# A hybrid decoder layer: GpSimd's elementwise work handed to VectorE and ScalarE in three stages, a factor read from PSUM, and copies moved behind a load

## The chip, the cores and the metric

The kernel runs on one core of one Trainium2 chip. The time is the device time in microseconds of one execution; of several runs the median is taken. In the profile the engines are PE (TensorE; PEld is its loading of weights), DVE (VectorE), ACT (ScalarE), POOL (GpSimd) and SP (SyncE, which in this kernel issues all DMAs). Each engine works through its own list of instructions in order, and instructions on different engines wait for each other through semaphores.

## The reference

One layer of a hybrid decoder on 1024 tokens of width 1024, then a final RMSNorm, all in float32:

```python
h = h + concat(gated_delta_net(rmsnorm(h)), s5(rmsnorm(h))) @ w_out   # one in-projection
h = h + cross_attention(rmsnorm(h), rmsnorm(mem))                     # 4 heads, 256 memory tokens
h = h + (silu(hn @ w_gate) * (hn @ w_up)) @ w_down                    # hn = rmsnorm(h), 2816 wide
return rmsnorm(h)
```

The parts that the change touches are these. In the delta net, q, k and v pass a causal convolution of width 4 and a silu; each of 4 heads then works with gates `g` (decay) and `beta`, of which cumulative sums, `exp(g_cum)` and `exp(-|g_cum[i] - g_cum[j]|)` are needed. Its output is normalised, `o * rsqrt(mean(o*o) + eps) * gain * silu(z)`. The S5 branch ends in `y = gelu(y)`, `y = y * sigmoid(y @ w_glu + b_glu)`. The last RMSNorm multiplies each token's row by one factor and each column by a gain.

## The kernel before, in words

Activations lie with the channel on the partitions and the tokens along the row, in tiles of 128 partitions and 512 columns. Matrix products are made to keep float32's accuracy: each operand is split into a high part and a low part (`split`, L62 on ACT makes the high one, L63 on DVE or POOL the low one), and a product is three matmuls (`mm3`, L79 to L81) that accumulate in one PSUM bank. PSUM has eight banks, handed out by pools: `pm` (three banks, tiles named mm) is there all the time; `p5` (one bank, tiles named aux) until the S5 gate is done; `pda`, `pdb`, `p6`, `ps`, `po` in single stages; `pa` (five banks, aux again) from the out-projection on. A tile that is asked for while its pool's banks are in use waits until the readers of the oldest are done.

The order of the instructions on each engine isn't the order of the program text: a planner simulates the engines with its own costs and lays each instruction where it expects its inputs and its buffer to be ready. `issue_after(x)` forces what is written under it to stand behind x on x's engine. All loads and stores go through `load` (L54), so they all stand in SP's queue.

The stages, with the lines that matter:

1. The in-projection of S5's inputs, then `s5_setup` and `s5_pre`, which make each channel group's impulse response in HBM (TD). `s5_toeplitz` copies it, from HBM to HBM in eight DMAs of 256 KB, into shifted form (TT), which `s5_in` reads much later.
2. `zab` makes z and the gates' raw values; `gates` computes g and beta, sums g with two small matmuls into p5 (gc and, transposed, gr) and stores gr to HBM (gD). `mem_prep` norms the memory tokens: a column sum and a row broadcast, both in p5, and eight scalings (L826) that read that bank.
3. For each of four heads: `in_tile` projects k, q and v; its convolution (L489 to L492) accumulates in p5. `dn_a` loads gD as a broadcast to all partitions (d_Qg), subtracts on POOL (L583), takes Abs and Exp on ACT (L584 to L586), and copies two single columns, al and kdc, on DVE (L588, L589). Then come transposes (L595) and products on PE in the pool pda.
4. `dn_seq` runs the recurrence over 8 chunks of tokens; `dn_tail` (L791 to L799) norms a chunk's output: squares and sums on ACT, a reciprocal root in ten tiny DVE operations (L85 to L89), a product with the root on DVE, a product with silu(z), the tile sz, on POOL, transposes on PE. The S5 recurrence runs beside it.
5. `glu`, the S5 gate: eight products, in p5 and p6 by turns; ACT takes the sigmoid into an SBUF tile (L909), DVE adds the two halves of y (L910), POOL multiplies (L911).
6. Out-projection, cross-attention, the two wide feed-forward products.
7. The down-projection, five chunks of 512 features with Winograd's 7 products for 2 x 2 blocks. `down_acts` loads a chunk's activations, subtracts (L1255) and splits them (L63) into seven operands; of these, the splits number 1, 3, 7 and 6 and one subtraction, two tiles each, are on POOL, ten operations of 128x512 for each chunk. `down_weights` splits weights, half of them on POOL (wlo from wb). `down_products` adds each product to hT or Q on DVE (L1325).
8. The rest of the features, and the final norm, for 512, 256 and 256 tokens. `final` broadcasts the factor with matmuls (L143) into a PSUM bank, copies it to SBUF on ACT (L139), and multiplies eight tiles, even ones on DVE (L1380), odd ones on POOL (L1378); a store follows each pair.

Of the kernel before, what the change touches and what calls it, by code (L numbers as in the profile page):

```python
# [9 lines left out]
F32 = mybir.dt.float32  # L10
F32R = mybir.dt.float32r
I32 = mybir.dt.int32
AF = mybir.ActivationFunctionType
ALU = mybir.AluOpType
# [4 lines left out]
P = 128  # L19
NT = 1024  # L20
HT = 512
# [24 lines left out]
class Kernel:  # L46
# [478 lines left out]
    def gates(self, ab, cv):  # L525
# [25 lines left out]
        ps = self.p5.tile([P, HT], F32, name="aux")  # L551
# [5 lines left out]
        ps = self.p5.tile([P, HT], F32, name="aux")  # L557
# [8 lines left out]
    def dn_a(self, hd, q, k, dp, dx):  # L566
# [15 lines left out]
        self.load(Qg, self.gD.rearrange("(c h) p -> h c p", h=4)[hd:hd + 1].to_broadcast(sh))  # L582
# [5 lines left out]
        v.tensor_copy(out=al, in_=Qg[:, :, P - 1])  # L588
        v.tensor_copy(out=kdc, in_=E[:, :, P - 1])  # L589
# [190 lines left out]
    def dn_tail(self, c, po, dq, xs):  # L780
# [14 lines left out]
        v.tensor_tensor(out=on, in0=po, in1=ro.unsqueeze(2).to_broadcast(sh), op=ALU.mult)  # L795
        g.tensor_tensor(out=on, in0=on, in1=sz, op=ALU.mult)
# [7 lines left out]
    def mem_prep(self, cv):  # L804
# [12 lines left out]
        ps = lambda: self.p5.tile([P, HT], F32, name="aux")  # L817
# [72 lines left out]
    def glu(self, q8, xs):  # L890
# [9 lines left out]
        for h in range(2):  # L900
            yh, yl = y8[h]
            out = []
            for m in range(4):
# [4 lines left out]
                sg, yy = T("yr"), T("yy", 8)  # L908
                self.a.activation(out=sg, in_=ps, func=AF.Sigmoid, bias=self.bglu[:, m:m + 1])  # L909
                self.v.tensor_tensor(out=yy, in0=yh[:, m].bitcast(F32), in1=yl[:, m].bitcast(F32), op=ALU.add)  # L910
                self.g.tensor_tensor(out=yy, in0=yy, in1=sg, op=ALU.mult)  # L911
# [319 lines left out]
    def down_acts(self, c, raw=None):  # L1231

        v, g = self.v, self.g
# [23 lines left out]
        def first(n):  # L1257
            if n == 0:
                put(1, b11, self.g)
                put(2, b21, self.v)  # L1260
            elif n == 1:
                put(3, b22, self.g)
                sub(v, b11, b12, b11)
                sub(g, b12, b22, b12)
            elif n == 2:
                put(7, b12, self.g)
                sub(v, b22, b22, b11)
                sub(v, b21, b21, b22)

        def rest(lw):  # L1270
# [4 lines left out]
            put(6, b22, self.g)  # L1275
# [94 lines left out]
    def final(self, o, rs):  # L1370

        n = o.stop - o.start
        rb = self.tmp.tile([P, HT], F32, name="res", bufs=2)[:, 0:n]
        self.rowbc(rs, n // P, rb)
        for m in range(KD):
            dst = self.out_rows(m, o)
            if m % 2 == 1:
                self.g.tensor_tensor(out=dst, in0=dst, in1=rb, op=ALU.mult)  # L1378
            else:
                self.v.scalar_tensor_tensor(out=dst, in0=dst, scalar=self.gain(4, m), in1=rb, op0=ALU.mult, op1=ALU.mult)  # L1380
# [27 lines left out]
    def emit(self, ctx):  # L1408
# [32 lines left out]
        with pool("cv", bufs=1) as cv:  # L1441
# [12 lines left out]
            with pool("s5t", "right", bufs=1) as tp:  # L1454
# [3 lines left out]
                self.s5_toeplitz(S)  # L1458
# [4 lines left out]
            with psum("pda", 1) as self.pda, psum("pdb", 2) as self.pb:  # L1463
                with pool("dx", "right", bufs=1) as dx:
                    for hd in range(4):
                        k, q = self.in_tile(4 + hd, cv), self.in_tile(hd, cv)
                        B = self.dn_a(hd, q, k, dp, dx)
                        v_ = self.in_tile(8 + hd, cv)
# [211 lines left out]
```

## Time and profile before

| | us |
|---|---|
| median of 3 runs | 1603.62 |
| lowest and highest run | 1600.15, 1607.66 |
| the profiled execution | 1605.2 |
| its span, first to last instruction | 1603.2 |
| busy in it: PE, PEld | 1457.7, 1218.8 |
| busy in it: DVE, ACT, POOL | 1188.9, 634.7, 655.9 |

A row of the profile's groups reads: line, engine, operation, tile written and tiles read, shapes, count, then busy time in us, mean duration in ns, and the idle time of the engine just before these instructions, with what ended it. A row of a timeline reads: start, duration, engine, line, operation, tiles, shapes, count, and in brackets the idle time before it and whose work ended it. The granted clock of PE is given as a share of full speed. SPq stands for the queue of SyncE. Stretches are in us from the start of the span.

### The profile page before, as it was taken

The page shows a single profiled execution, that of the slowest core. Times are in us where ns is not written, and L with a number is a line of the kernel's source. Part 1 is how long each engine was busy: PE and PEld are TensorE (multiplying, and loading weights), DVE is VectorE, ACT ScalarE, POOL GpSimd, SP SyncE. Part 2 cuts the span into 40 slices and gives each one's busy share as a digit, 9 for nine tenths or more (in the row PEclk, how much of TensorE's full clock was granted, in tenths as well). Part 3 has the DMA queues.
Part 4 walks back from the last instruction along what each step waited for, and adds up shares of the span by engine and source line. Part 5 has one row for each costly group of instructions (what it writes and reads, how often), then busy time and mean ns, then how long its engine had stood idle before and what let it go on. Part 6 is the DMA issues. An engine that isn't in the chain of part 4 may idle for free.

```text
span 1603.2 us, 20926 instructions
## 1 busy us (share of the span) xinstructions
PE 1457.7 (91%) x7326; PEld 1218.8 (76%) x7326; DVE 1188.9 (74%) x2164; ACT 634.7 (40%) x1137; POOL 655.9 (41%) x475
## 2 busy tenths in 40 slices
PE   6887699996978788999999999999999998999985
PEld 4787488886877576878888788888888886777864
DVE  8969489886699797775546697666666668899886
ACT  5222353452544563454443442333333334533322
POOL 6175234324552416620010443333333347766544
PEclk9999899997989988999999999999999999999997
DMA  7256454548688152245524414444444357444302
GB/s 224 80 164 199 134 133 124 140 119 293 213 291 265 47 197 105 79 131 171 171 92 165 144 33 145 149 142 139 145 137 137 112 168 251 149 146 150 126 10 105
DMA packets 146616, 237.49 MB, mean 148 GB/s; under 512 B 12464, under 2 KB 79440, under 8 KB 143952
## 3 DMA queue, kind: packets, MB, share of 16 engines
q1 hardware_dynamic: 146512, 236.17, 45.7%
q8 instruction: 57, 0.93, 0.2%
q14 instruction: 47, 0.39, 0.1%
HBM read 169.69 MB, written 68.53 MB: 149 GB/s over the span
## 4 chain that ended last, share of the span: by engine, by line
PE 53%; DVE 24%; DMA 9%; issue 5%; ACT 4%; POOL 3%; SPq 1%; DVEq 0%; POOLq 0%; ACTq 0%
PE aux L81 9%; PE aux L79 9%; PE aux L80 9%; PE mm L81 8%; PE mm L79 8%; PE mm L80 8%; DVE aux L491 2%; DVE wlo L63 1%; DVE d_R L675 1%; DMA s_wb<-in_s5bT 1%; DVE s_S L398 1%; POOL wlo L63 1%; DVE hT L1380 1%; DMA d_R<-LD 1%; DMA wraw<-in_w_xk 1%
## 5 line engine op out<-in xcount | busy, mean ns | idle before, releaser
L62 ACT ACTIVATE whi<-wraw 128x1024 fp32r<-128x1024 f32 (+2 forms) x152 | 139.7, 922 | 202.3 <-PE mm L80 67.3
L79 PE MATMUL mm<-AH,whi 128*128 128x512 f32 x448 | 178.4, 399 | 1.4 <-DVE hT L1325 1.4
L81 PE MATMUL mm<-AH,wlo 128*128 128x512 f32 x432 | 170.9, 396 | 0.0
L80 PE MATMUL mm<-AL,whi 128*128 128x512 f32 x408 | 161.3, 396 | 0.0
L150 POOL TENSOR_TENSOR acc<-acc,sq 128x512 f32<-128x512 f32 (+1 forms) x41 | 53.1, 1295 | 212.9 <-ACT sq L149 212.1
L63 DVE TENSOR_TENSOR wlo<-wraw,whi 128x1024 fp32r<-128x1024 f32 (+1 forms) x76 | 97.9, 1290 | 33.2 <-ACT whi L62 33.1
L1204 POOL TENSOR_TENSOR sg<-sg,ca 128x512 f32<-128x512 f32 x40 | 58.2, 1456 | 144.1 <-DVE sg L1197 92.7
L63 POOL TENSOR_TENSOR wlo<-wraw,whi 128x1024 fp32r<-128x1024 f32 x28 | 67.8, 2422 | 115.8 <-ACT whi L62 98.8
L79 PEld LDWEIGHTS mm<-AH,whi 128*128 128x128 f32 x448 | 84.6, 189 | 20.9 <-DVE hT L1325 2.9
L81 PEld LDWEIGHTS mm<-AH,wlo 128*128 128x128 f32 x432 | 81.5, 189 | 18.3 <-issue 0.4
L80 PEld LDWEIGHTS mm<-AL,whi 128*128 128x128 f32 x408 | 77.1, 189 | 16.6
L80 PE MATMUL aux<-AL,whi 128*128 128x512 f32 x216 | 85.0, 393 | 0.7 <-POOL AL L63 0.7
L79 PE MATMUL aux<-AH,whi 128*128 128x512 f32 x176 | 69.7, 396 | 0.0
L62 ACT ACTIVATE wlo<-graw 128x512 fp32r<-128x512 f32 x62 | 38.8, 626 | 62.7 <-PE aux L81 53.1
L81 PE MATMUL aux<-AH,wlo 128*128 128x512 f32 x160 | 63.4, 396 | 0.0
L491 DVE SCALAR_TENSOR_TENSOR aux<-pre,convw,aux 128x512 f32<-128x512 f32 x72 | 54.1, 751 | 8.3 <-ACT aux L489 7.5
L1202 ACT ACTIVATE ca<-ca 128x512 f32<-128x512 f32 x40 | 25.3, 633 | 83.5 <-DVE ca L1197 83.0
L63 POOL TENSOR_TENSOR wlo<-wb,whi 128x768 fp32r<-128x768 f32 x19 | 39.8, 2094 | 42.3 <-ACT whi L62 42.3
L81 PE MATMUL aux<-AH,whi 128*128 128x512 f32 x136 | 53.4, 392 | 0.0
L80 PEld LDWEIGHTS aux<-AL,whi 128*128 128x128 f32 x216 | 40.6, 188 | 10.6 <-POOL AL L63 1.4
L63 DVE TENSOR_TENSOR wlo<-graw,wlo 128x512 fp32r<-128x512 f32 x40 | 46.0, 1150 | 2.2 <-ACT wlo L62 2.2
L79 PE MATMUL aux<-AH,wlo 128*128 128x512 f32 x120 | 47.3, 394 | 0.0
(713 smaller groups left out, 4678.2 us busy)
## 6 DMA issues: line engine op xcount, KB each, us to landing
graw<-in_w_up SPq DMA_DIRECT2D x22, 512.0 KB
acc<-in_w_down SPq DMA_DIRECT2D x42, 256.0 KB
actD<-sg SPq DMA_DIRECT2D x40, 256.0 KB
WD<-acc SPq DMA_DIRECT2D x40, 256.0 KB
wraw<-in_w_in SPq DMA_DIRECT2D x16, 512.0 KB
d_X<-XD SPq DMA_DIRECT2D x8, 1024.0 KB
wraw<-AD SPq DMA_DIRECT2D x16, 512.0 KB
wraw<-VD SPq DMA_DIRECT2D x16, 512.0 KB
```

The costliest lines, as they stand in the source:

```text
L62: self.a.activation(out=hi, in_=src, func=AF.Copy)
L63: return (eng or self.v).tensor_tensor(out=lo, in0=src, in1=hi.bitcast(F32), op=ALU.subtract)
L79: mm(ps, wh, xh, start=first, stop=False)
L80: mm(ps, wh, xl, start=False, stop=False)
L81: mm(ps, wl, xh, start=False, stop=last)
L150: eng.tensor_tensor(out=acc, in0=acc, in1=tmp, op=ALU.add)
L398: v.tensor_tensor_scan(out=Zs[:, k, q], data0=self.m8[:, 2 * b + q:2 * b + q + 1].to_broadcast([P, P]), data1=Z[:, k, q], initial=0.0, op0 ...
L491: v.scalar_tensor_tensor(out=acc, in0=pre[:, 1 + i:1 + i + HT], scalar=cw(i), in1=acc, op0=ALU.mult, op1=ALU.add)
L675: tt(out=R[:, i, :, 0:i], in0=R[:, i, :, 0:i], in1=X[:, :, 0:i], op=ALU.mult)
L1202: A.activation(out=r, in_=r, func=AF.Silu)
L1204: g.tensor_tensor(out=r, in0=r, in1=sg[o], op=ALU.mult)
L1380: self.v.scalar_tensor_tensor(out=dst, in0=dst, scalar=self.gain(4, m), in1=rb, op0=ALU.mult, op1=ALU.mult)
```

## The change

- `gates` and `mem_prep` take their PSUM banks from pm in place of p5.
- The two column copies of `dn_a`, al and kdc, run on ACT.
- `dn_tail` multiplies by sz first, on DVE from PSUM, and by the root after it, on ACT in four operations of 128 columns.
- `glu` leaves the sigmoid in its PSUM bank, and DVE multiplies by it there.
- The ten operations of `down_acts` that were on POOL are on DVE.
- `final` reads the factor from its PSUM bank for the DVE operations; POOL keeps the tiles 1, 3 and 5, with ACT's copy of the factor, and tile 7 goes to DVE.
- The copies of `s5_toeplitz` are written behind the first head's `dn_a`, and queued on SP behind its load of d_Qg.

```diff
 gates
-        ps = self.p5.tile([P, HT], F32, name="aux")
+        ps = self.pm.tile([P, HT], F32, name="mm")
         self.te.matmul(ps[:, 0:32], self.UT, g_.rearrange("p a b -> p (a b)"), start=True, stop=True)
...
-        ps = self.p5.tile([P, HT], F32, name="aux")
+        ps = self.pm.tile([P, HT], F32, name="mm")
         self.te.matmul(ps[0:32, 0:P], g_.rearrange("p a b -> p (a b)"), self.UT, start=True, stop=True)
 dn_a
-        self.load(Qg, self.gD.rearrange("(c h) p -> h c p", h=4)[hd:hd + 1].to_broadcast(sh))
+        self.first = self.load(Qg, self.gD.rearrange("(c h) p -> h c p", h=4)[hd:hd + 1].to_broadcast(sh))
...
-        v.tensor_copy(out=al, in_=Qg[:, :, P - 1])
-        v.tensor_copy(out=kdc, in_=E[:, :, P - 1])
+        A.activation(out=al, in_=Qg[:, :, P - 1], func=AF.Copy)
+        A.activation(out=kdc, in_=E[:, :, P - 1], func=AF.Copy)
 dn_tail
-        v.tensor_tensor(out=on, in0=po, in1=ro.unsqueeze(2).to_broadcast(sh), op=ALU.mult)
-        g.tensor_tensor(out=on, in0=on, in1=sz, op=ALU.mult)
+        v.tensor_tensor(out=on, in0=po, in1=sz, op=ALU.mult)
+        for i in range(4):
+            A.activation(out=on[:, i], in_=on[:, i], func=AF.Copy, scale=ro[:, i:i + 1])
 mem_prep
-        ps = lambda: self.p5.tile([P, HT], F32, name="aux")
+        ps = lambda: self.pm.tile([P, HT], F32, name="mm")
 glu
-                sg, yy = T("yr"), T("yy", 8)
-                self.a.activation(out=sg, in_=ps, func=AF.Sigmoid, bias=self.bglu[:, m:m + 1])
+                yy = T("yy", 8)
+                self.a.activation(out=ps, in_=ps, func=AF.Sigmoid, bias=self.bglu[:, m:m + 1])
...
-                self.g.tensor_tensor(out=yy, in0=yy, in1=sg, op=ALU.mult)
+                self.v.tensor_tensor(out=yy, in0=yy, in1=ps, op=ALU.mult)
 down_acts
-        v, g = self.v, self.g
+        v = g = self.v
...
-                put(1, b11, self.g)
+                put(1, b11, g)
...
-                put(3, b22, self.g)
+                put(3, b22, g)
                 sub(v, b11, b12, b11)
                 sub(g, b12, b22, b12)
...
-                put(7, b12, self.g)
+                put(7, b12, g)
...
-            put(6, b22, self.g)
+            put(6, b22, g)
 final
+        ps = self.pa.tile([P, HT], F32, name="aux")
+        self.row_sums(rs, n // P, ps)
         rb = self.tmp.tile([P, HT], F32, name="res", bufs=2)[:, 0:n]
-        self.rowbc(rs, n // P, rb)
+        self.a.activation(out=rb, in_=ps[:, 0:n], func=AF.Copy)
...
-            if m % 2 == 1:
+            if m in (1, 3, 5):
                 self.g.tensor_tensor(out=dst, in0=dst, in1=rb, op=ALU.mult)
+            elif m == 7:
+                self.v.tensor_tensor(out=dst, in0=dst, in1=ps[:, 0:n], op=ALU.mult)
             else:
-                self.v.scalar_tensor_tensor(out=dst, in0=dst, scalar=self.gain(4, m), in1=rb, op0=ALU.mult, op1=ALU.mult)
+                self.v.scalar_tensor_tensor(out=dst, in0=dst, scalar=self.gain(4, m), in1=ps[:, 0:n], op0=ALU.mult, op1=ALU.mult)
 emit
-                self.s5_toeplitz(S)
...
                         B = self.dn_a(hd, q, k, dp, dx)
+                        if hd == 0:
+                            with self.tc.issue_after(self.first.ins):
+                                self.s5_toeplitz(S)
```

## The prediction

> **What bounds the kernel now.** I read the page first: the spans of the engines and the chain of waits.
>
> ```profile
> span 1603.2 us, 20926 instructions
> PE 1457.7 (91%) x7326; PEld 1218.8 (76%) x7326; DVE 1188.9 (74%) x2164; ACT 634.7 (40%) x1137; POOL 655.9 (41%) x475
> PE 53%; DVE 24%; DMA 9%; issue 5%; ACT 4%; POOL 3%; SPq 1%; DVEq 0%; POOLq 0%; ACTq 0%
> ```
>
> TensorE carries the chain; all it leaves idle is 1603.2 - 1457.7 = 145.5 us, so an edit pays only where it closes a hole in PE, or in the tail. The second view, busy time by stretch, tells where the holes are near the change (columns: stretch, length, then busy time of PE, PEld, DVE, ACT, POOL, granted clock, DMA share, GB/s).
>
> ```profile
> 160.00:200.00 40.00, 24.79 (x109) 19.78 (x108) 18.07 (x45) 11.89 (x16) 11.61 (x7) 0.83 0.46 137
> 200.00:240.00 40.00, 40.00 (x206) 33.69 (x205) 31.90 (x63) 20.77 (x40) 16.00 (x8) 1.00 0.49 131
> 520.00:560.00 40.00, 28.89 (x163) 24.33 (x161) 28.43 (x62) 19.57 (x46) 18.72 (x14) 0.92 0.15 46
> 1345.50:1385.00 39.50, 37.78 (x156) 30.09 (x155) 26.44 (x28) 22.75 (x39) 23.33 (x15) 0.95 0.64 234
> 1385.00:1424.50 39.50, 39.50 (x172) 31.83 (x171) 37.92 (x46) 15.96 (x24) 26.80 (x15) 1.00 0.48 156
> 1424.50:1464.00 39.50, 39.18 (x169) 31.47 (x168) 37.18 (x45) 15.40 (x23) 25.10 (x14) 1.00 0.46 147
> 1464.00:1503.50 39.50, 39.19 (x169) 31.50 (x168) 37.35 (x44) 16.29 (x24) 28.17 (x16) 1.00 0.39 128
> 1500.00:1603.00 103.00, 77.73 (x377) 64.75 (x375) 78.54 (x125) 28.77 (x55) 54.17 (x43) 0.88 0.21 73
> ```
>
> So the front of the delta-net stage has 15.2 us of hole and is followed by a stretch where PE is full; the stretch of the gates of S5 has 11.1; the down-projection has none to give (PE 39.2 to 39.5 of 39.5, with DVE at 37 to 38 close behind); the tail has 25.
>
> **The front (gates, mem_prep, dn_a, the response copies).** The timelines by engine and the chain of waits (its DMA rows: start, time to landing) show who is late:
>
> ```profile
> 168.22 0.27 DVE L560 COPY gr<-aux 32x128 f32<-32x128 f32 x1
> 169.47 5.57 SPq L54 DMA_DIRECT2D TT<-TD  x7
> 175.14 4.25 DMA gD<-gr
> 179.44 4.98 DMA d_Qg<-gD
> 186.70 1.06 ACT L584 ACTIVATE d_E<-d_E 128x1024 f32<-128x1024 f32 x1 [10.46 <-POOL d_E L583]
> 188.79 0.22 DVE L588 COPY dn_al<-d_Qg 128x8 f32<-128x8 f32 x1 [13.67 <-ACT d_Qg L586]
> 188.92 1.65 DVE L826 SCALAR_TENSOR_TENSOR res<-res,gains,aux 128x256 f32<-128x256 f32 x4
> 192.05 0.99 DVE L589 COPY d_kdc<-d_E 128x8 f32<-128x8 f32 x1
> 192.97 2.32 DVE L491 SCALAR_TENSOR_TENSOR aux<-pre,convw,aux 128x512 f32<-128x512 f32 x3
> 195.97 1.12 PE L595 MATMUL da<-cst,it 128*128 128x128 f32 x4 [14.66 <-ACT it L492]
> ```
>
> The gates' row gr is ready at 168.5, but its store stands in SP's queue behind the response copies and goes at 175.14; the broadcast d_Qg follows at 179.44 and lands at 184.4, and only then do POOL and ACT make E. DVE meanwhile stands 13.67 us before dn_al, a copy of 0.22 us, in order. Behind it wait mem_prep's scalings L826, which read the single p5 bank; behind that bank wait the convolutions of the k tile, though their input has been ready since this row:
>
> ```profile
> 160.50 0.67 DVE L480 TENSOR_TENSOR pre<-mm,rbx 128x512 f32<-128x512 f32 x1
> ```
>
> PE ends this in 14.66 us of idleness. Three edits cut the loop at three places. The copies go behind the broadcast: the store issues at 168.5, 6.6 us sooner, and its landing (4.25 us with the rings full, 175.14 to 179.4) and the broadcast's (5.0) are also shorter without 8 copies of 256 KB ahead; by how much no row shows, so E comes between 6.6 us (nothing more) and 11 us sooner (2 us off each landing); I take 10. dn_al and d_kdc go to ACT, right behind the exponentials that they read, at about 0.2 us each (the nearest row of that size is DVE's 0.22), so DVE's 13.67 us wait is gone. And p5 is left to the convolutions: a half tile, 2.32 us on DVE and less on ACT, can start at 168 in place of 192, so the k tile is there before PE comes to L595 at 181.3. What is late next is d_kdc: it ends at 193.0 now, 3 us before L595, and would be there at about 181, with L595 at 181.3; PE's projections, which fill it after L595 now, cover what is missing.
>
> The price: mem_prep holds one of three mm banks from about 173 until DVE has done L826, and the projections have two meanwhile; silu and exponential now alternate on ACT, two more table loads, hidden in its 10.46 us wait. The SP queue waits for the landing of gr, then issues eight copies for some 6 us; behind them stand a weight load, kD and XD stores. Their bytes still fill the rings (share 1.02 below, over 1 from 170 to 180):
>
> ```profile
> 175.00:180.00 5.00, 5.00 (x23) 4.05 (x22) 0.12 (x1) 1.06 (x1) 0.00 (x0) 1.00 1.02 307
> 185.00:190.00 5.00, 0.00 (x0) 0.00 (x0) 1.21 (x4) 3.14 (x4) 3.98 (x2) 0.52 0.04 4
> ```
>
> The hole also drops the granted clock to 0.52; what comes right after it, such as the transposes L595 with their 1.12 us, can gain with a clock that stays up, 1 us at a guess from that row. Bounds: -6.6 and -16 (14.66 and that 1); I take **-13**, nearer the far end because each of the three links is cut by itself. For the later heads dn_al's waits end too, but beside a PE that is full (40.00 of 40.00 from 200 to 240): **-1**, between 0 and -2.
>
> **dn_tail and the S5 gate.** These rows are from 500 to 557 us:
>
> ```profile
> L911 POOL TENSOR_TENSOR yy<-yy,yr 128x512 f32<-128x512 f32 x8 | 10.8, 1356 | 9.2 <-ACT yr L909 8.2 <-DVE d_w4b L88 0.9
> L910 DVE TENSOR_TENSOR yy<-AH,AL 128x512 f32<-128x512 f32 x8 | 5.1, 685 | 0.0
> L791 ACT ACTIVATE d_R<-po 128x128 f32<-128x128 f32 x16 | 4.2, 278 | 10.5 <-PE po L777 8.0 <-DVE d_w4b L88 2.5
> 547.28 1.14 DVE L89 SCALAR_TENSOR_TENSOR d_ro<-d_w4b,d_ro 128x4 f32<-128x4 f32 x1
> L796 POOL TENSOR_TENSOR d_R<-d_R,d_L 128x512 f32<-128x512 f32 x5 | 6.8, 1350 | 15.2 <-issue 11.2 <-DVE d_R L795 4.0
> 554.62 1.11 PE L799 MATMUL po<-cst,d_R 128*128 128x128 f32 x4 [6.15 <-POOL d_R L796]
> ```
>
> DVE's step of four columns took 1.14 us beside a POOL operation; dn_al, eight columns wide, took 0.22 alone. The last tail ends with PE idle for 6.15 us before its transposes at 554.62. After, POOL is silent here; two such steps of the root lose 0.9 us each, and DVE's product before POOL's (about 0.69, as L910) and POOL's 1.35 give way to four ACT scalings of 0.28, 1.1 together, the product with sz now being made beside the root: -1.8 - 0.9 = -2.7 on the path to PE. Of the eight gate products that move to DVE at 0.68, one may fall into that tail: +0.7. The sigmoid stays in p5 or p6 until DVE has read it, 0.7 us and DVE's queue longer, and the next product but one of PE waits for that bank: nothing where DVE is free (28.43 of 40 busy), else 0.7 for each of eight. Lower bound -6, nearly the whole hole; upper bound -2.7 + 0.7 + 5.6 = +3.6, called +3; I take **-2**, from the rows without a stall.
>
> **The down-projection's operands.** Ten operations of 128x512 for each chunk leave POOL for DVE. In the four stretches from 1345.5 to 1503.5:
>
> ```profile
> L63 POOL TENSOR_TENSOR wlo<-wb,whi 128x768 fp32r<-128x768 f32 x16 | 33.9, 2117 | 36.9 <-ACT whi L62 36.9
> L63 POOL TENSOR_TENSOR AL<-sq,AL 128x512 fp32r<-128x512 f32 x8 | 14.7, 1848 | 1.5 <-ACT AL L62 1.5
> L1325 DVE TENSOR_TENSOR Q<-Q,aux 128x512 f32<-128x512 f32 x37 | 24.8, 677 | 3.9 <-PE aux L81 3.9
> L1255 DVE TENSOR_TENSOR res<-res,fsg 128x512 f32<-128x512 f32 x8 | 11.8, 1476 | 0.1
> L63 DVE TENSOR_TENSOR o<-acc,o 128x512 fp32r<-128x512 f32 x8 | 8.2, 1060 | 4.2 <-PE mm L80 4.2
> ```
>
> L1325, with an operand in PSUM, takes 0.677 in POOL's company; L1255 and L63, both operands in SBUF, take 1.06 to 1.48 against 0.685 alone (L910 above). DVE has six such groups here, 47 operations and 59.7 us, a mean of 1.27 (the dearest and the cheapest are quoted): 59.7 - 47 x 0.685 = 28 us of waiting for POOL. Of POOL's 103.4 us (23.33 + 26.80 + 25.10 + 28.17) the weight splits, 33.9, stay, and with them a third of the waiting: 19 us go, 40 x 0.68 = 27 come, 8 us more on DVE, 2 for each stretch. DVE's idle time there is 13.1, 1.6, 2.3 and 2.2. So it just fits, and PE, which sets the pace, stays at 39.5 for each: **0**, bounds -2 (holes of PE) and +9 (no relief: 27 less the 19.2 idle).
>
> **The final norm.**
>
> ```profile
> L1380 DVE SCALAR_TENSOR_TENSOR hT<-hT,gains,res 128x512 f32<-128x512 f32 x4 | 6.9, 1787 | 1.9 <-ACT res L139 1.9
> L1380 DVE SCALAR_TENSOR_TENSOR hT<-hT,gains,res 128x256 f32<-128x256 f32 x8 | 7.3, 967 | 3.0 <-ACT res L139 3.0
> L139 ACT ACTIVATE res<-aux 128x256 f32<-128x256 f32 x2 | 0.8, 384 | 7.5 <-PE aux L143 7.5
> L150 POOL TENSOR_TENSOR acc<-acc,sq 128x256 f32<-128x256 f32 x10 | 7.3, 728 | 11.4 <-ACT sq L149 11.0
> 1579.40:1584.60 5.20, 5.13 (x24) 5.16 (x25) 2.44 (x9) 3.35 (x9) 2.92 (x4) 0.50 0.31 119
> ```
>
> The first call has 512 columns, the second and third 256; each is followed by work that waits for it, or by the end. With the factor in PSUM an operation costs what L826 (four in 1.65 us) and L1325 show: 0.41 at 256 columns, 0.68 at 512, and needn't wait for ACT's copy, 0.4. First call: 6.9 + 0.4 become 5 x 0.68 = 3.4: -3.9. Second, half of 7.3: 3.65 + 0.4 become 2.05: -2.0. Third: ACT's copy and POOL's three at the price of L150, 0.4 + 3 x 0.73 = 2.6, in place of 4.05: -1.5. If the first saving closes the hole of PE behind it, the clock stays up where it fell to 0.50 and PE ran 5.1 us: 0 to -2.6. Of -7.4 to -10 I take **-9**.
>
> The Trainium skill (TensorE: Matmul & The Clock Gate, What's actually happening) lets the clock fall to a half after one idle window of some 3.4 us. By that rule a closed hole would bring all 2.6, and the sum would be 1579; the 0.50 after the hole agrees.
>
> **Sum.** -13 - 1 - 2 + 0 - 9 = -25. The profiled execution took 1605.2 us (span 1603.2), 1.6 over the median of 1603.62 of the runs: 1605.2 - 25 = **1580**. All lower bounds together give 1569 (-16 - 2 - 6 - 2 - 10 = -36), all upper ones 1603 (-6.6 + 0 + 3 + 9 - 7.4 = -2).
>
> **Rivals.** *The front hole moves and doesn't close*: the weight load behind the moved copies, or ACT held in order before d_E, keeps PE idle for 8 us, and the front gives -5: 1605.2 - 5 - 1 - 2 - 9 = 1588. For it: the full rings quoted. Against: in the trace nothing waits for the loads that stand behind the copies, only for d_Qg and the k tile, which now stand ahead. The Trainium skill (DMA: Bandwidth & Descriptors, Queues, rings and completion order) says that a queue's descriptors are consumed in ring order, so whatever is issued behind the copies waits for them; the 4.25 us of gr's store, which is small, agree. *Nothing to measure*: the order in which the planner lays the front's work on ACT and DVE keeps the loop, the front gives -3, the down stage takes its +9 and the norm gives -9: 1602. *DVE becomes the bound of the down-projection*: if the ten operations cost 1.3 us each, as their neighbours do now, and these aren't relieved, a stretch needs 37.5 + 13 = 50.5 us of DVE against 39.5 of PE: +11 for each of three, +33, and with -22 from front and norm 1616. It decides once DVE's need passes 39.5, two us from now. Against it: the lock follows POOL's load, and that falls by two thirds.
>
> **Chances.** Forecast 0.60 (its own range 1571 to 1587), moved hole 0.23, nothing 0.09, DVE bound 0.08. Runs of this kernel spread over 0.5%, which is the least that can be told from no change. The first two are faster by more: 0.83; same 0.09; slower 0.08. The range for eight in ten, 1568 to 1597, takes in the second case and most of the bounds.
>
> **What would show it.** Right: gD stored before the copies, no PE wait over 3 us before L595, clock 1.00 there; L1255 and L63 near 0.7 in the down stage with DVE under 39 of 39.5; final-norm operations at 0.41 and 0.68. Wrong: PE waits for L1325 or for a split in the down stage; PE waiting on a weight load near 190; products of the S5 gate spaced by DVE.

## The result, and the profile after

The changed kernel took 1586.5 us, the median of 4 runs (1585.08 to 1589.19); the kernel before took 1605.64 us beside it (4 runs, 1600.15 to 1613.67). The ratio of the two is 0.985, with a 95% interval from 0.982 to 0.988: 19 to 29 us less. The profiled execution took 1586.9 us, 18.3 less than the one that the prediction was worked out from. The forecast was 1580.

The page of the kernel after, its engines and the chain of waits:

```profile
span 1585.2 us, 20917 instructions
PE 1463.2 (92%) x7326; PEld 1221.1 (77%) x7326; DVE 1185.2 (75%) x2217; ACT 647.7 (41%) x1179; POOL 544.6 (34%) x406
PE 59%; DVE 19%; DMA 10%; issue 4%; ACT 3%; POOL 3%; SPq 1%; POOLq 0%; DVEq 0%; ACTq 0%
```

What PE leaves idle fell from 145.5 to 122.0 us. POOL lost 111 us of work, and DVE isn't busier although 61 of POOL's operations went to it (its count rose by only 53 because eight column copies went to ACT): that is the relief that the prediction counted on, and more of it.

Where the time went is seen by comparing the two traces at equal work, because the planner has laid PE's work in another order. In the next table each matmul counts with the lower quartile of the start-to-start spacings of its kind in both traces; the work done at a time is the sum over the matmuls already begun, of 1354 us in all.

| work done, us | stage | time before | after against before |
|---|---|---|---|
| 90 | S5 setup | 137.6 | +2.1 |
| 120 | gates, first projections | 171.5 | +13.3 |
| 140 | first head | 207.9 | -2.8 |
| 240 | last head | 315.8 | +9.8 |
| 400 | S5 gate | 539.8 | +8.3 |
| 440 | out-projection | 613.0 | -9.4 |
| 1120 | before the down-projection | 1314.7 | -5.5 |
| 1320 | end of the down-projection | 1529.2 | -10.1 |
| all | end | 1603.2 | -18.0 |

So up to the first head the front gives 3 us, the later heads lose 12.6, and what is won stands in three places: between the S5 gate and the out-projection (-18), in the down-projection (-5) and in the final norm (-8). A difference of 4 us in such a table is noise: a kernel that differs from the kernel before only in its last 35 us (e_final below) is 4.5 us behind it at work 140. All four kernels below with the front unchanged are 2 to 5 us behind it there; against them the front gives 5 to 8 us by the first head.

The stretches of the kernel after, in the columns of the prediction's second view, first the front in slices of 5 us:

```profile
150.00:155.00 5.00, 2.30 (x9) 1.51 (x10) 4.97 (x12) 3.17 (x5) 0.81 (x1) 0.68 1.03 349
155.00:160.00 5.00, 4.41 (x19) 3.11 (x17) 4.79 (x8) 3.11 (x4) 3.92 (x2) 0.50 0.78 221
160.00:165.00 5.00, 1.23 (x5) 1.26 (x6) 4.22 (x29) 0.23 (x1) 0.00 (x0) 0.50 0.70 234
...
185.00:190.00 5.00, 5.00 (x27) 4.20 (x26) 0.00 (x0) 3.22 (x3) 1.72 (x1) 1.00 1.00 255
...
520.00:560.00 40.00, 35.24 (x204) 29.88 (x202) 28.80 (x64) 26.34 (x60) 6.11 (x4) 1.00 0.36 120
```

The old hole at 185 is closed, with the clock at 1.00; new ones stand around 150 and 160, and PE runs at a granted clock of 0.50 to 0.68 from 150 to 165 us. The first is a wait of 3.29 us for an operation of the gates on DVE, up to 151.87 (2.19 us in the kernel before); the second is the 4.36 us in the next view. The stretch of the S5 gate, 28.89 of 40 busy before, is at 35.24. The timelines by engine show what is late in the front:

```profile
162.15 0.42 SPq L54 DMA_DIRECT2D gD<-gr  x1
163.78 1.19 PE L822 MATMUL mm<-cst,rsm 128*128 128x128 f32 x4 [4.36 <-DVE rsm L89]
165.00 1.66 DVE L827 SCALAR_TENSOR_TENSOR res<-res,gains,mm 128x256 f32<-128x256 f32 x4 [0.73 <-PE mm L822]
174.21 0.67 DVE L98 TENSOR_TENSOR s_W<-s_G 128x512 f32<-128x512 f32 x1
174.91 0.38 SPq L54 DMA_DIRECT2D SD<-s_W  x1
177.71 0.38 SPq L54 DMA_DIRECT2D d_Qg<-gD  x1
178.14 8.62 SPq L54 DMA_DIRECT2D TT<-TD  x8
184.80 1.92 POOL L583 TENSOR_TENSOR d_E<-d_Qg,gc 128x1024 f32<-128x1024 f32 x1 [3.35 <-DMA TT<-TD]
188.90 1.04 PE L595 MATMUL da<-cst,it 128*128 128x128 f32 x8
```

The gates' row is stored at 162.15, 13 us earlier than before and ahead of the copies, as predicted. But the broadcast goes only at 177.71 (179.44 before). In SP's queue it stands behind the store of the S5 setup's last s_W, and s_W is late for two reasons: DVE now makes mem_prep's scalings (L827) first, and three of the steps that lead to s_W (L94 to L96) take 1.54 to 1.67 us each, beside POOL's splits of mem_prep's tiles, against 0.69 before. E begins at 184.80. The view of SP's waits for 155 to 200 us names both sides of the store, 9.9 us before it until DVE is done (put down to DVE's next operation, L484) and 2.2 us behind it until it has landed:

```profile
SPq L54 <- DVE pre L484: 9.9, 1, 9.9
SPq L54 <- DMA SD<-s_W: 2.2, 1, 2.2
```

### The profile page after: what moved, and what is told of

The parts are those of the page before. It is cut to its first block, busy times and chain, and to the rows that moved or that the text cites. A ratio compares the mean times of both kernels' runs of the same rounds, so it can differ in the third digit from the quotient of the medians.

```text
span 1585.2 us, 20917 instructions
## 1 busy us (share of the span) xinstructions
PE 1463.2 (92%) x7326; PEld 1221.1 (77%) x7326; DVE 1185.2 (75%) x2217; ACT 647.7 (41%) x1179; POOL 544.6 (34%) x406
## 4 chain that ended last, share of the span: by engine, by line
PE 59%; DVE 19%; DMA 10%; issue 4%; ACT 3%; POOL 3%; SPq 1%; POOLq 0%; DVEq 0%; ACTq 0%
PE mm L79 9%; PE mm L81 9%; PE mm L80 9%; PE aux L81 9%; PE aux L80 9%; PE aux L79 9%; PE db L689 1%; SPq L54 1%; DMA s_wb<-in_s5bT 1%; DVE aux L491 1%; DVE wlo L63 1%; DMA s_wa<-acoD 1%; DMA wraw<-in_w_out 1%; DMA d_M<-yD 1%; DVE AL L66 1%
## 5 line engine op out<-in xcount | busy, mean ns | idle before, releaser
L81 PE MATMUL mm<-AH,wlo 128*128 128x512 f32 x432 | 173.0, 401 | 0.0
L63 DVE TENSOR_TENSOR wlo<-wraw,whi 128x1024 fp32r<-128x1024 f32 (+1 forms) x76 | 100.4, 1323 | 31.6 <-ACT whi L62 31.2
L63 POOL TENSOR_TENSOR wlo<-wraw,whi 128x1024 fp32r<-128x1024 f32 x28 | 68.5, 2446 | 124.4 <-ACT whi L62 120.3
L81 PEld LDWEIGHTS mm<-AH,wlo 128*128 128x128 f32 x432 | 82.4, 191 | 18.5
L63 POOL TENSOR_TENSOR wlo<-wb,whi 128x768 fp32r<-128x768 f32 x19 | 38.9, 2048 | 127.3 <-ACT whi L62 119.6
L491 DVE SCALAR_TENSOR_TENSOR aux<-pre,convw,aux 128x512 f32<-128x512 f32 x72 | 54.0, 750 | 27.0 <-ACT aux L489 25.9
L81 PE MATMUL aux<-AH,wlo 128*128 128x512 f32 x160 | 63.5, 397 | 0.0
L81 PE MATMUL aux<-AH,whi 128*128 128x512 f32 x136 | 53.6, 394 | 0.0
L80 PE MATMUL aux<-AL,wlo 128*128 128x512 f32 x120 | 47.1, 393 | 0.0
```

Source lines behind the costliest of these rows:

```text
L63: return (eng or self.v).tensor_tensor(out=lo, in0=src, in1=hi.bitcast(F32), op=ALU.subtract)
L80: mm(ps, wh, xl, start=False, stop=False)
L81: mm(ps, wl, xh, start=False, stop=last)
L491: v.scalar_tensor_tensor(out=acc, in0=pre[:, 1 + i:1 + i + HT], scalar=cw(i), in1=acc, op0=ALU.mult, op1=ALU.add)
```

## The experiments

All ratios are to the kernel before on the same chip, with 95% intervals; its median there lay between 1610 and 1612 us, and microseconds below are the ratio times that. Kernels named e_ are the kernel before with a part of the change, those named a_ the kernel after with a part undone or something added, those named m_ the kernel after cut down to the three parts that proved to matter.

### One part at a time

**e_front**: gates and mem_prep on pm, al and kdc on ACT, the response copies behind d_Qg.

```diff
-        ps = self.p5.tile([P, HT], F32, name="aux")
+        ps = self.pm.tile([P, HT], F32, name="mm")
...
+        A.activation(out=al, in_=Qg[:, :, P - 1], func=AF.Copy)
...
+                            with self.tc.issue_after(self.first.ins):
+                                self.s5_toeplitz(S)
```

> The kernel before with only the edits of the front: gates and mem_prep take their PSUM banks from pm, al and kdc are copied on ACT, the response copies stand behind the load of d_Qg. Theory (the hole of the front is moved, not closed): in the changed kernel the gates' and mem_prep's tiles stand ahead of the projections in pm's three banks, PE waits 4.36 us for mem_prep's root and runs at a granted clock of 0.50 to 0.61 from 150 to 170 us, and the later heads lose some 10 us more in holes of 1.6 to 2.4 us with the clock down to 0.54 behind them; so this kernel is not faster than the kernel before: between -2 and +9 us. Rival (the prediction's step): the front gives -13 and the later heads -1, and what the changed kernel loses after 200 us comes from its other edits or from the planner's order with them: -14 us.

Measured: 0.9968 (0.9954 to 0.9982), -5.2 us. Neither: the prediction's -14 is out, and the theory's "not faster" too. Where these 5 us come from is seen two sections below.

**e_tailglu**: dn_tail and the S5 gate.

```diff
+        v.tensor_tensor(out=on, in0=po, in1=sz, op=ALU.mult)
+        for i in range(4):
+            A.activation(out=on[:, i], in_=on[:, i], func=AF.Copy, scale=ro[:, i:i + 1])
...
+                self.a.activation(out=ps, in_=ps, func=AF.Sigmoid, bias=self.bglu[:, m:m + 1])
+                self.v.tensor_tensor(out=yy, in0=yy, in1=ps, op=ALU.mult)
```

> The kernel before with only dn_tail (product with sz on DVE, root on ACT) and the S5 gate (sigmoid left in PSUM, product on DVE) changed. Theory: the 6.15 and 4.12 us in which PE waited for the last tail and the gate's products go, and with them the time at a lower clock behind them; between 530 and 563 us the changed kernel won some 9 us at equal matmul work, so -8 to -10 us. Rival (the prediction's step): -2 us, the rest of what the changed kernel won there being holes that its other edits had moved before this stage: -2 us or less.

Measured: 1.0004 (0.9987 to 1.0022), +0.6 us. The hole before the last tail's transposes did shrink, from 6.15 us to the 4.17 of this row of PE's timeline, so most of the prediction's -2.7 for that path is there; it doesn't reach the end. The theory's -8 to -10 is out, and the prediction's -2 lies at the edge of the interval (-2.1 to +3.5).

```profile
557.72 1.35 PE L800 MATMUL po<-cst,d_R 128*128 128x128 f32 x4 [4.17 <-ACT d_R L797]
```

**e_down**: as it ran, this kernel moved only the two subtractions to DVE, not the ten operations that its expectation names; the eight splits stayed on POOL.

```diff
-        v, g = self.v, self.g
+        v = g = self.v
```

> The kernel before with only the ten operations of down_acts moved from POOL to DVE. Theory (the operations of DVE that run beside POOL get shorter, from 1.06 to 1.48 us to about 0.68, and PE stays full): -2 to -4 us, since the changed kernel won 2 to 4 us between the first and the last matmul of the down-projection. Rival 1 (the prediction's term): 0, the gain of the changed kernel there being its other order of loads. Rival 2 (DVE, at 39.5 busy of 39.5 in the changed kernel, is the bound): over +5 us.

Measured: 1.0037 (1.0018 to 1.0056), +6.0 us: slower. The groups of DVE and POOL from 1390 to 1510 us, then a stretch there, then the waits of PE there say why:

```profile
L1255 DVE TENSOR_TENSOR sq<-fsg,sq 128x512 f32<-128x512 f32 x6 | 11.8, 1962 | 0.0
L63 POOL TENSOR_TENSOR AL<-fsg,AL 128x512 fp32r<-128x512 f32 x6 | 10.4, 1744 | 0.0
```

```profile
1430.00:1470.00 40.00, 37.98 (x161) 29.57 (x160) 36.75 (x46) 13.92 (x20) 19.34 (x12) 1.00 0.42 135
```

```profile
PE mm L79 <- DVE hT L1325: 3.3, 3, 1.2
PE aux L81 <- DVE wlo L63: 2.7, 3, 1.5
```

The moved subtraction costs DVE 1.96 us, not 0.68, as long as POOL's splits stand beside it, and PE loses 2 us of every 40 to DVE.

**e_down10**: all ten operations.

```diff
-        v, g = self.v, self.g
+        v = g = self.v
...
-                put(1, b11, self.g)
+                put(1, b11, g)
...
-            put(6, b22, self.g)
+            put(6, b22, g)
```

> The kernel before with all ten operations of down_acts on DVE. (The earlier kernel e_down moved only the subtraction, two of the ten; the eight splits stayed on POOL.) Theory (relief comes only when POOL's splits of activations are gone too): the moved operations and their neighbours fall to 0.68 us, where the two moved alone took 1.96 us, DVE is full and PE too, 39.5 of 39.5: -4 us to 0, and so 6 to 10 us under e_down, which lost 6 (ratio 1.0037). Rival (DVE is the bound of this stage, and the changed kernel only escapes it by what its other edits do): as e_down or worse, +5 us or more.

Measured: 0.9952 (0.9931 to 0.9973), -7.7 us, 14 us under the kernel that moves two. The subtraction shown for that kernel, one of the moved splits, and the same stretch:

```profile
L1255 DVE TENSOR_TENSOR sq<-fsg,sq 128x512 f32<-128x512 f32 x6 | 6.8, 1127 | 0.0
L63 DVE TENSOR_TENSOR AL<-sq,AL 128x512 fp32r<-128x512 f32 x6 | 4.1, 679 | 0.0
```

```profile
1430.00:1470.00 40.00, 40.00 (x174) 32.41 (x173) 40.00 (x58) 15.65 (x23) 10.82 (x5) 1.00 0.47 156
```

DVE is full, 40.00 of 40, and so is PE. The subtraction takes 1.13 us where it took 1.96. Of the eleven groups of such operations (L63 and L1255, 128x512) from 1390 to 1510 us seven are at 0.68 us and four at 0.86 to 1.13; their mean is 0.79, against 1.23 in e_down and 1.22 in the kernel before. The relief is real but not whole, and the gain is larger than the theory's -4 to 0.

**e_final**: the final norm.

```diff
+        self.row_sums(rs, n // P, ps)
+        self.a.activation(out=rb, in_=ps[:, 0:n], func=AF.Copy)
...
+                self.v.scalar_tensor_tensor(out=dst, in0=dst, scalar=self.gain(4, m), in1=ps[:, 0:n], op0=ALU.mult, op1=ALU.mult)
```

> The kernel before with only the final norm changed (DVE reads the factor in its PSUM bank, POOL has three tiles). Theory: the three calls give what the changed kernel won from the end of the down-projection on, -7 us: the operations at 0.41 and 0.68 us as predicted, but DVE still stands behind ACT's copy of the factor, which the prediction had let it pass (0.4 us for each call), and PE's clock is down to a half in the last column sums. Rival (the prediction's sum): -9 us.

Measured: 0.9945 (0.9928 to 0.9962), -8.9 us. The interval, -11.6 to -6.1, holds the theory's -7 and the prediction's -9 alike.

The four parts (e_down10 for the down-projection) sum to -5.2 + 0.6 - 7.7 - 8.9 = -21.2 us; together they measured -24 (-29 to -19). No interaction is needed to explain the total.

### What of the front matters

Each of these is the kernel after with one edit of the front undone.

**a_p5**: gates and mem_prep on p5.

```diff
-        ps = self.pm.tile([P, HT], F32, name="mm")
+        ps = self.p5.tile([P, HT], F32, name="aux")
```

> The kernel after with gates and mem_prep on p5 again, all else as changed. Theory (the tiles in pm cost PE the hole of 4.36 us and some 20 us at half a clock from 150 to 170 us, 12 us at equal work, while the loop in front of the k tile is already cut by the copies on ACT): 5 to 12 us faster than the kernel after, ratio to the kernel before 0.978 to 0.982. Rival (the prediction's: p5 is what the convolutions wait for): the hole of 10 to 14 us before the k tile's transposes comes back beside the other one gone, ratio 0.985 to 0.990.

Measured: 0.9929 (0.9898 to 0.996), 13 us slower than the kernel after: the theory is out, and the mechanism is the rival's, the prediction's, at a price above its range. The hole at 150 to 165 us is gone (PE 5.00 of 5.00 from 155 to 170), and the one before the k tile's transposes is back, in PE's timeline:

```profile
195.87 1.12 PE L595 MATMUL da<-cst,it 128*128 128x128 f32 x4 [11.35 <-ACT it L492]
```

Its five runs lie between 1588.26 and 1601.82 us, and the profiled one is the fastest, 1.4 us above the profiled execution of the kernel after. So this trace shows that the hole is back, but not where the 13 us are lost.

**a_dvecopies**: al and kdc on DVE.

```diff
-        A.activation(out=al, in_=Qg[:, :, P - 1], func=AF.Copy)
-        A.activation(out=kdc, in_=E[:, :, P - 1], func=AF.Copy)
+        v.tensor_copy(out=al, in_=Qg[:, :, P - 1])
+        v.tensor_copy(out=kdc, in_=E[:, :, P - 1])
```

> The kernel after with al and kdc on DVE again. Theory (with mem_prep out of p5 the copies that wait on DVE delay the k tile's convolution as before, and the first products of each head): 3 to 8 us slower than the kernel after, ratio to the kernel before 0.988 to 0.990. Rival (the copies are not what is late once the convolutions have p5 to themselves, and the two table loads they cost ACT, with the holes of the second and third head behind ACT, go): 0 to 5 us faster than the kernel after, 0.982 to 0.985.

Measured: 0.9859 (0.9831 to 0.9887), as the kernel after (0.985): the copies on ACT bought nothing that shows, though the theory's least, 0.988, is still inside the interval. With mem_prep out of p5, dn_al waits 3.47 us on DVE in place of 13.67, and the hole of PE before L595 stays closed.

**a_tt**: the response copies in their old place.

```diff
-                        if hd == 0:
-                            with self.tc.issue_after(self.first.ins):
-                                self.s5_toeplitz(S)
```

> The kernel after with the response copies where they were, behind the S5 setup and without an order on SP. Theory (the move bought nothing: in the changed kernel the broadcast d_Qg stood behind the store of s_W, not behind the copies, went at 177.71 against 179.44, and took 7 us to land against 5 with the copies right behind it): the same as the kernel after within 3 us, ratio 0.983 to 0.987. Rival (the prediction's: the store of gr waits for the copies again): 4 to 7 us slower, 0.988 to 0.990.

Measured: 0.9838 (0.9811 to 0.9865): the theory holds, the move bought nothing. SP and POOL in its timelines:

```profile
162.82 0.42 SPq L54 DMA_DIRECT2D gD<-gr  x1
168.09 4.87 SPq L54 DMA_DIRECT2D TT<-TD  x7
175.61 0.39 SPq L54 DMA_DIRECT2D SD<-s_W  x1
178.78 0.38 SPq L54 DMA_DIRECT2D d_Qg<-gD  x1
184.66 1.92 POOL L583 TENSOR_TENSOR d_E<-d_Qg,gc 128x1024 f32<-128x1024 f32 x1 [2.51 <-DVE pre L480]
```

Here the planner stores gr before the copies by itself, since with pm the row is ready sooner. The broadcast goes behind s_W's store as in the kernel after, and E begins at the same 184.7.

### Where the front's 5 us are

The place was found by summing the holes of PE over 1 us by stretch. Between 530 and 625 us they fall into groups that follow one edit, and with them goes the longest POOL operation of 540 to 640 us (e_down, with p5, is like the first three: 22.5 and 11.83):

| kernel | gates, mem_prep | PE's holes 100 to 240 | 360 to 530 | 530 to 625 | longest POOL operation |
|---|---|---|---|---|---|
| before | p5 | 26.9 | 25.2 | 23.3 | 11.82 |
| e_final | p5 | 29.2 | 28.7 | 22.8 | 11.82 |
| e_down10 | p5 | 27.9 | 29.2 | 22.4 | 10.92 |
| e_tailglu | p5 | 25.9 | 29.0 | 18.7 | 7.64 |
| a_p5 | p5 | 24.6 | 25.8 | 19.5 | 7.60 |
| e_front | pm | 24.7 | 33.6 | 8.1 | 5.05 |
| after | pm | 20.4 | 31.6 | 8.8 | 2.25 |
| a_tt | pm | 22.2 | 32.0 | 7.8 | 2.25 |
| a_dvecopies | pm | 23.3 | 30.7 | 7.8 | 2.25 |
| a_min | pm | 23.7 | 32.5 | 8.0 | 5.14 |

With pm the front's holes are 4 us less in the mean (while the clock falls there), the S5 stage's 1.5 to 8.4 more, and the end of the stage loses 10 to 15 us of hole. The S5 branch now ends with the delta net's last tail instead of before it (last gate matmul at 557.3, last tail's transposes at 554.5; before, 548.5 and 555.7), so each fills the other's waits. And an operation of POOL isn't held up any more. POOL and DVE in the kernel before, by their timelines:

```profile
596.17 0.68 DVE L944 TENSOR_TENSOR res<-res,sq 128x512 f32<-128x512 f32 x1
596.77 0.68 DVE L952 TENSOR_TENSOR res<-res,AH 128x512 f32<-128x512 f32 x1
596.99 11.82 POOL L63 TENSOR_TENSOR wlo<-fsg,wlo 128x512 fp32r<-128x512 f32 x1 [4.30 <-ACT wlo L62]
...
607.72 1.64 DVE L956 TENSOR_TENSOR res<-res,AL 128x512 f32<-128x512 f32 x1
```

and the same operation in the kernel after:

```profile
593.51 0.68 DVE L63 TENSOR_TENSOR AL<-res,AH 128x512 fp32r<-128x512 f32 x1
593.74 1.60 POOL L63 TENSOR_TENSOR wlo<-fsg,wlo 128x512 fp32r<-128x512 f32 x1 [2.85 <-ACT wlo L62]
594.12 1.77 DVE L983 TENSOR_TENSOR wraw<-wraw 128x512 f32<-128x512 f32 x1
```

A split of 1.6 us took 11.82 while DVE ran one operation behind the other at 0.60 us, and ended when one of DVE's gave way and took 1.64. (Spans on POOL are rough, but its next operation begins at 608.77.) A dense run of DVE alone isn't enough for this: in the kernel after, the split at 593.74 comes through behind one operation of such a run, and DVE's next takes 1.77; in the kernel before, a split at 620.17 does the same in 1.61. What decides between the two isn't shown. PE's hole of 9.50 us at 599 was this: the next row of the chain of waits of the kernel before is a product L81 on PE at 608.87. Why the planner lays DVE's run so in the kernels with p5 wasn't taken apart.

By equal work e_front is 5 to 7 us ahead of the four kernels with the old front at the first head, 10 to 12 behind them at the S5 gate, and 4 to 7 ahead where the kernel before is at 625 us. So what the front wins is lost by the later heads and the S5 stage, and the 5 us that are left at the end are won between the S5 gate and the out-projection.

### Smaller, and with the k projection first

**a_min**: only pm, down_acts and the final norm; the other edits are undone with the lines shown above.

> The kernel after with three edits undone: the copies al and kdc on DVE, the response copies in their old place, dn_tail and the S5 gate as before; what stays is gates and mem_prep on pm, down_acts on DVE and the final norm. Theory (only these three parts carry the gain; alone they measured -5 for the front, -8 and -9, and the others nothing): as the kernel after or a little faster, -20 to -28 us, ratio 0.982 to 0.987. Rival (the copies and the S5 gate are worth something together with the rest: the sum of the parts alone, -21, is less than the -24 of the kernel after): 4 us or more slower than the kernel after, 0.9875 or more.

Measured: 0.9867 (0.9847 to 0.9888), -21.4 us, against 0.985 for all: the theory's range. The interval doesn't tell it from the kernel after, and it holds the rival's 0.9875 too.

**a_kfirst**: the first head's k projection ahead of gates and mem_prep.

```diff
+            k0 = self.in_tile(4, cv)
             self.gates(zab, cv)
             mem = self.mem_prep(cv)
...
-                        k, q = self.in_tile(4 + hd, cv), self.in_tile(hd, cv)
+                        k, q = self.in_tile(4 + hd, cv) if hd else k0, self.in_tile(hd, cv)
```

> The kernel after with the first head's k projection written ahead of gates and mem_prep, so that its two tiles come before theirs in pm's three banks and PE has projections to do while DVE makes the gates and the root. Theory (the order of the tiles in pm is what empties PE from 148 to 165 us: holes of 3.29 and 4.36 us and the clock at a half): the holes go, 8 to 12 us at equal work at 170 us, and of it 0 to 8 us reach the end, since in the kernels with pm the stage's end stood against other work; ratio to the kernel before 0.978 to 0.985. Rival (the holes come from DVE's and ACT's order there, not from the banks): they stay within 2 us, ratio 0.985.

Measured: 0.9835 (0.9817 to 0.9854), not to be told from the kernel after. Two of its stretches:

```profile
155.00:160.00 5.00, 5.00 (x28) 4.13 (x27) 4.60 (x15) 0.00 (x0) 2.37 (x1) 1.00 0.84 192
170.00:175.00 5.00, 1.11 (x4) 0.71 (x4) 4.96 (x8) 4.64 (x6) 3.28 (x2) 0.50 0.05 17
```

As the theory says, the order of the tiles in pm emptied PE: with k's two tiles ahead it is full up to 164 us. But then it has almost nothing until mem_prep's factor at 181, since q's tiles stand behind mem_prep's. The theory's 8 to 12 us at equal work are there for a moment (12 ahead of the kernel after where the kernel before is at 160 us) and gone at 171.5, where this kernel is 4 behind; the holes didn't go, from 160 to 185 they are 14.4 us against 4.4.

**m_kfirst**: the same edit on a_min.

> As the kernel with the k projection first, but on the kernel with only pm, down_acts and the final norm changed. Theory (both changes are independent): the ratio of that smaller kernel less what the k projection first gives on the kernel after, 0.978 to 0.984. Rival (the planner's order of the delta-net stage decides more than either): any ratio between 0.978 and 0.995, with the holes at other places than in the kernel with the k projection first.

Measured: 0.9788 (0.9768 to 0.9809), median 1578.65 us: faster than both kernels. It gives 13 us on a_min and 2 on the kernel after, so the two aren't independent, as the rival says. Its front has the same hole (0.00 busy from 170 to 175); the gain lies in shorter holes in the S5 stage (23.3 us from 360 to 530, against 32.5 in a_min).

**m_kq**: q first as well.

```diff
             self.gates(zab, cv)
+            q0 = self.in_tile(0, cv)
             mem = self.mem_prep(cv)
```

> As the smaller kernel with the k projection first, and the first head's q projection too stands ahead of mem_prep (k projection, gates, q projection, mem_prep). Theory (PE is empty whenever the tiles that come next in pm's order wait for DVE: with k first it had work until 164 us and then 16 us at half a clock, up to mem_prep's factor at 178; with q first as well the 48 matmuls of q fill that): the holes between 160 and 185 us shrink from 13.9 to 5 us or less with the clock at 1.00, and up to 8 us of it reach the end: ratio 0.974 to 0.979. Rival (what is won in the front is taken up by the wait for the first S5 operands near 380 us and the end of the delta-net chain): the holes shrink, the time stays, 0.979 to 0.984.

Measured: 0.988 (0.9848 to 0.9911). Both miss on the time: it is slower than m_kfirst by 15 us. Between 160 and 185 the holes do fall to 5.2 us, but 8.74 and 4.31 us of new ones stand at 184 and 194, before mem_prep's column sums and the products of k, and those from 360 to 530 are 33.4 us again, against 23.3. Each time the front's hole was filled at one place, it stood at the next.

m_kfirst and m_kq differ from their neighbours by 13 and 15 us, more than any part of the change is worth, though they only put the same projections at another place. So a part's few us, the front's -5 above all, may belong to the order that the planner found as much as to the edit; no run here separates the two.

## Why the prediction was right, and where it wasn't

The sum, -25 us, is near the -24 (-29 to -19) measured, but in part by luck: the front gave 9 us less than forecast and the down-projection 8 us more, and these two errors make up for each other.

| term | predicted | measured alone |
|---|---|---|
| front and later heads | -14 | -5.2 (-7.4 to -2.9) |
| dn_tail, S5 gate | -2 | +0.6 (-2.1 to +3.5) |
| down-projection's operands | 0 | -7.7 (-11.1 to -4.4) |
| final norm | -9 | -8.9 (-11.6 to -6.1) |

**Front.** The 14.66 us hole closed, and that pm does it is shown by a_p5. Four steps failed. "The projections have two meanwhile" treated the banks as free to be taken by whoever is ready; pm's tiles are taken in the order of the program, so the projections wait behind mem_prep's tile until DVE has made its root, and PE stands 4.36 us. Together with the 3.29 us wait ahead of it this leaves PE 15 us at 0.50 to 0.68 of its clock. "I take 10" for E: it begins at 184.80, as before, because the broadcast waits for a store that the prediction hadn't looked at, s_W's, and because it took longer from its issue to E, not shorter: 7.1 us with the copies queued right behind it, 5.0 before, 5.9 in a_tt. That the copies slow it is likely but not shown. And the copies to ACT are worth nothing that shows (a_dvecopies): once the convolutions have a bank, dn_al holds up nothing that matters. The two more table loads of ACT are there, 18 against 16, but not because of the copies (a_dvecopies has 18 too, a_p5 16), and not hidden: the one at 187.83, 1.28 us, stands between E's two activations. The rival "the front hole moves and doesn't close" described the front better, with -5 as its price, though the place and the cause were others: the hole of 14.66 us did close, and what that wins the later stages lose again.

The fourth step is the later heads' term, -1, the one most out of size. By equal work they lose 12.6 us (from -2.8 to +9.8). This is PE in the kernel after over three heads, with holes of 2.37 us at 231 and 1.64 at 303 among its idle time:

```profile
208.00:320.00 112.00, 104.94 (x583) 89.46 (x582) 92.47 (x204) 50.02 (x93) 43.50 (x23) 0.95 0.47 124
```

The kernel before has PE busy for 110.29 us of this stretch at a clock of 1.00, and a_p5 for 110.73 at 1.00: 5.4 us of idle time more and some 5 us of lower clock go with pm, and with the order that the planner finds for it.

**dn_tail and S5 gate.** Of the 2.7 us on the path 2.0 are there (6.15 to 4.17; ACT's scalings take 0.39 us each in the kernel after, not 0.28). The step that failed is that the path sets the end: the time doesn't move within 3 us, and the change's gain at this place belongs to pm. One of the signs of being wrong came here: in the kernel after a product of the gate waits 1.77 us for DVE's yy, up to 538.12.

**Down-projection.** The mechanism was right: DVE's operations got shorter (0.79 us in the mean against 1.22) and DVE just fits; "DVE under 39 of 39.5" was a shade too low, it is full. The size was off: the term was put at 0, and the holes of PE that it closes at 2 us, from the four stretches after 1345.5. The waits of PE from 1335 to 1545 us, first in the kernel before, then in e_down10:

```profile
PE aux L79 <- ACT o L62: 5.3, 1, 5.3
PE aux L79 <- DVE hT L1325: 1.7, 1, 1.7
PE mm L79 <- DVE hT L1325: 1.4, 3, 0.8
PE aux L79 <- DVE Q L1325: 1.0, 1, 1.0
PE aux L80 <- POOL AL L63: 0.7, 1, 0.7
```

```profile
PE aux L79 <- ACT o L62: 4.6, 1, 4.6
PE mm L79 <- DVE Q L1325: 1.1, 1, 1.1
PE mm L79 <- DVE hT L1325: 0.3, 1, 0.3
PE aux L79 <- DVE hT L1325: 0.2, 1, 0.2
```

That is 10.1 against 6.2 us, 3.9 less, with waits before 1345 among them; by equal work from 1120 to 1320 e_down10 wins 5.1. The rest of the -7.7 (-11.1 to -4.4) isn't accounted for. The rival that DVE becomes the bound was near in another sense: e_down, with two operations moved, is its first step, and lost 6 us.

**Final norm.** The operations cost what was predicted, by the timelines of the second call in the kernel after:

```profile
1572.55 0.38 ACT L1377 ACTIVATE res<-aux 128x256 f32<-128x256 f32 x1 [0.58 <-PE aux L143]
1572.97 1.65 DVE L1385 SCALAR_TENSOR_TENSOR hT<-hT,gains,aux 128x256 f32<-128x256 f32 x4 [1.53 <-ACT res L1377]
```

Four of DVE's take 1.65 us, and three of POOL's 2.09. One step failed: DVE "needn't wait for ACT's copy" of the factor. It starts behind the copy in all three calls (1572.97 here, the copy ending at 1572.93), and the profile names the copy as what it waited for, though both only read. The Trainium skill (PSUM — Partial Sum Buffer, PSUM bank collisions raise a hardware error) says that the compiler's scheduler puts any two instructions of different engines on the same bank and the same 32 partitions one behind the other, reads and writes alike; the rows agree. It takes back the 0.4 us that the sum had counted for each of the first two calls. The term "0 to -2.6" for the clock came true: the hole of PE behind the first call, the first row (the kernel before), shrinks to 0.67 us, and the stretch behind it, at a clock of 0.50 before, runs at 1.00, the second row (the kernel after):

```profile
1579.47 0.66 PE L120 MATMUL aux<-ones,acc 128*128 128x64 f32 x2 [4.47 <-DVE hT L1368]
1563.00:1568.00 5.00, 4.33 (x38) 4.16 (x37) 3.87 (x12) 3.21 (x9) 3.45 (x5) 1.00 0.98 364
```

In e_final the hole is 1.27 us and the clock from 1577 to 1587 is 1.00. The kernel after gives part of this back in its second call, where two column sums take 0.53 us against 0.33 before.

Of the signs named, these came: gD stored before the copies, the clock at 1.00 before L595, L1255 and L63 near 0.7 (0.79 in the mean), the norm at 0.41 and 0.68. This one didn't: no wait of PE over 3 us before L595.

## What to carry to other kernels

A tile handed out in program order from a small pool puts everything that asks later behind its readers; before moving a tile to a pool that is "there all the time", look at who is next in that pool and how long the new tile is held. Moving a few operations off POOL can cost more than moving none or all: what is dear is both engines reading SBUF at once, so count what stays. And a hole in front of a full stretch isn't a gain until the work behind it can end sooner; compare the traces at equal work, not at equal place, before crediting it.

## What the runs showed of the hardware that was not expected

A POOL operation can be held for far longer than one DVE operation: 11.82 us against 1.60, through a run of DVE operations with both operands in SBUF, one every 0.60 us. The Trainium skill (SBUF — State Buffer, Who interferes with whom) says that a DVE instruction with two SBUF inputs contends with one of POOL's that reads SBUF; the trace agrees. It shows POOL held through eighteen such operations in this one case, while at other places of the same trace POOL got in behind the first.

The granted clock fell to a half behind a hole shorter than the rule that the prediction cites. These are stretches of the kernel after behind the 1.64 us hole at 302.9:

```profile
302.50:305.00 2.50, 0.86 (x9) 0.70 (x7) 2.50 (x2) 0.00 (x0) 2.50 (x2) 1.00 0.25 58
305.00:307.50 2.50, 2.50 (x16) 2.50 (x15) 2.50 (x3) 0.00 (x0) 1.56 (x1) 0.58 0.00 0
307.50:310.00 2.50, 2.50 (x11) 2.31 (x11) 2.50 (x3) 0.00 (x0) 0.00 (x0) 0.50 0.00 0
```

PE was busy 0.86 of 2.5 us, with the last of eight transposes and with matmuls of 64 columns, and then ran 5 us at 0.50 to 0.58 and 2.5 us more at 0.55, so a hole of 1.64 us cost about 3.4 more, by estimate (7.5 less 2.5 times 0.58, 0.50 and 0.55). The Trainium skill (TensorE: Matmul & The Clock Gate, What's actually happening) asks for an idle window of some 3.4 us; no idle stretch of that length is here.
